# One gate of the recurrence in seven-product form before the first branch projection, and two gates of the second branch at other places

## The chip, the cores and the metric

The kernel runs on one core of a Trainium2 chip. The metric is device time in microseconds; the median of three runs of the kernel before is 935.56 us (934.21 to 936.03). The profile shows one more execution, which took 935.83 us; its span, from the first to the last instruction that the trace shows, is 933.7 us, so 2.1 us lie around it. Engines are named as in the profile: PE (matmuls), DVE (VectorE), ACT (ScalarE), POOL (GpSimd) and SP (which issues the weight loads).

## The reference

A decoder block over 512 tokens and 16 meta tokens in front of them, width 1024, all in float32. Cut to what matters here:

```python
u = rmsnorm(h, mix_norm_w)
q, k, v, g_ret, lru_in, lru_gate, gate_a, gate_b = split(u @ w_in)
o = chunk_retention(rotary(q), rotary(k), v)
y_ret = (silu(g_ret) * o) @ w_branch_ret
r = rg_lru(causal_depthwise_conv(lru_in), ...)
y_lru = (gelu(lru_gate) * r) @ w_branch_lru
mixed = sigmoid(gate_a) * y_ret + sigmoid(gate_b) * y_lru
h = h + mixed @ w_out
h = h + swiglu(rmsnorm(h, ffn_norm_w))
out = rmsnorm(h, final_norm_w)[:, 16:]
```

## The kernel before

Every float32 operand of a product is split in two halves: `hi`, the value cast to PE's fast 32-bit form (ACT, line 290 for weights, line 421 for activations), and `lo`, what the cast lost (DVE, line 294 or 422; a few on POOL). Each product is then three matmuls, hi by hi, hi by the other's lo, and lo by hi.

A weight slab of 1024 by 256 comes in four quarters of 128 partitions by 512 columns (a11, a12, a21, a22). There are two ways to multiply by it. `plain` uses the four quarters as they are: with 256 tokens per matmul that is 4 quarters x 2 token halves x 4 blocks x 3 matmuls = 96 matmuls. `fast` is a seven-product (Strassen-Winograd) form: POOL makes four sums of quarters, s1 to s4 (`combine`, line 260); seven operands (s1, s3, a12, a11, s4, a22, s2) are split by ACT and DVE; PE does 7 x 4 x 3 = 84 matmuls against the activations' quarters and their own sums t1 to t4, in four PSUM regions z, w, y, x; in the middle ACT copies w and x out and DVE adds z and w (`pz`, line 393), and at the end ACT copies x again (`u2`, line 398) and DVE makes the four output quarters by two additions (lines 407 and 408). `plain_slab` says which slabs take which way.

`PLAN` gives the order of the stages: R0 to R3 (the retention's projections), A0 to A3 (the gates of the first branch), I0 to I3 (the recurrence's inputs, followed by the convolution), L0 to L3 (the recurrence's output gates: a projection and a Gelu), T0 to T3 (the recurrence's inner gates and the recurrence itself), B0 to B3 (the gates of the second branch), BR and BL (the two branch projections). In the trace, a slab of `w_in` has a number: I0 and I1 are 16 and 17, L0 to L3 are 20 to 23, A0 to A3 are 24 to 27, B0 to B3 are 28 to 31. I0, I1 and the A gates are `fast`; I2, I3, all L and all B are `plain`.

A convolution (`conv`, line 978 and three lines 980 for each of two halves, on DVE) reads the padded input `xp` and writes `c`, which ACT and DVE then split (lines 421 and 422, 128x528); the work is issued bit by bit between the matmuls (`tick`). `branch` multiplies four activations R0 to R3 (or Z0 to Z3), each of 128x1024 and each split before use, by four slabs; BR is 192 matmuls of 512 columns in two groups of four PSUM banks (`w_br0_*`, `w_br1_*`). BR also gives back the activations' sums t1 to t4, so that nothing `fast` can follow it.

Three things set the order. Each engine runs its own queue strictly in the order of the built program; a scheduler has made that order at build time from the order of the code. Buffers are rings: 8 raw quarters, 9 pairs of hi and lo, 4 sums, 8 PSUM banks; a cast to `hi` waits until PE has read the pair nine places earlier. All larger tiles (named b with a number) live in 32 slots of SBUF that are handed out first freed, first used; a tile waits for the last reader of the tile that had its slot.

Of the kernel before, what the change touches and what calls it, by code (L numbers as in the profile page):

```python
# [13 lines left out]
AF = mybir.ActivationFunctionType  # L14
# [6 lines left out]
SEQ = 512  # L21
# [41 lines left out]
FIRST_LOADS = "w0 x1 w1 m w2 w3 x2 x3"  # L63


PLAN = "R0 R1 R2 R3 A0 A1 A2 A3 I0 I1 BR T0 L0 I2 T1 L1 I3 L2 T2 B0 L3 T3 B1 B2 B3 BL"

PLAIN_R = "K0 G0 K1 K2 K3".split()
NORM = 2.0
# [41 lines left out]
class Slots:  # L111
# [12 lines left out]
    def get(self, n=SEQ, dt=F32):  # L124
        if n <= T and dt == F32:
            if self.halves:
                slot, i = self.halves.pop(0)
            else:
                slot, i = [*self.open(dt), 0], 0
                self.halves.append((slot, 1))  # L130
            slot[2] += 1
            t = slot[1][:, i * T:i * T + n]
            self.held[id(t)] = (t, slot, i)
        else:
            tag, mem = self.open(dt)
            t = mem[:, :n]
            self.held[id(t)] = (t, tag, None)
        return t
# [15 lines left out]
def hybrid_block(ctx: ExitStack, tc: tile.TileContext, a: dict):  # L154
# [10 lines left out]
    def bank(name):  # L165
        return ps.tile([P, 512], F32, tag="ps", name=name)
# [24 lines left out]
    Q, K, V, G, LI, LG, GA, GB = (4 * i for i in range(8))  # L191
# [4 lines left out]
    SLAB_OF = {"I": ("w_in", LI), "L": ("w_in", LG), "A": ("w_in", GA), "B": ("w_in", GB), "T": ("gates", 0)}  # L196
    for step in PLAN.split():
        if step in ("BR", "BL"):
            order += [(f"w_{step.lower()}", hf) for hf in range(2)]
        elif step[0] == "R":  # L200
            s = int(step[1])
# [12 lines left out]

    def plain_slab(key, i):
        if key == "w_in":
            return i in [{"Q": Q, "K": K, "G": G}[r[0]] + int(r[1]) for r in PLAIN_R] or LI + 2 <= i < GA or i >= GB
        return key == "w_fi" and i <= FIRST

    pieces = []  # L220
    for n, (key, i) in enumerate(order):
        if n == 0:
            pieces += PLAIN_V
        if key in ("w_br", "w_bl"):

            pieces += [(key, k // 2, k % 2 + 2 * (1 - i)) for k in range(KT)]
        elif plain_slab(key, i):
            pieces += [(key, i, c) for c in PLAIN]
        elif key == "w_v":
            pieces += [(key, j, c) for c in FAST for j in (i, i + 1)] if i else []  # L230
        elif key in ("w_in", "w_fi"):
            pieces += [(key, i, c) for c in FAST]
        elif key == "w_fo":
            pieces += [(key, i, c) for c in (2, 0, 3, 1)]
        else:
            pieces += [(key, i, c) for c in range(2 if key == "gates" else 4)]
    state = {"n": 0, "look": 0}

    def behind(ins, other):

        if other is not None:
            tc.add_manual_dep(ins.ins, other.ins.name, mybir.DependencyInfo(
                mybir.DependencyClass.NoSync, mybir.DependencyReason.DATA), reason="issue order")
        return ins
# [74 lines left out]
    def lookup(*args, **kw):  # L319
        state["table"] = behind(nc.scalar.activation(*args, **kw), state.get("table"))  # L320
# [56 lines left out]
    def fast(key, s, X, n, banks, name):  # L377

        z, w_, y, x = banks
        own = n == TH
        ws = small.tile([P, TH], F32, tag="ws", name=f"ws{name}{s}")
        pz = small.tile([P, 2, TH], F32, tag="pz", name=f"pz{name}{s}")
        u2 = small.tile([P, TH], F32, tag="u2", name=f"u2{name}{s}")
        part = lambda name: weights((key, s, name))[0]
        block(z, part("s1"), X["t1"], n, True)
        block(w_, part("s3"), X["t3"], n, own)
        block(y, part("a12"), X["b21"], n, True)  # L390
        block(x, part("a11"), X["b11"], n, own)
        nc.scalar.copy(ws[:, :n], w_)
        nc.vector.tensor_tensor(pz[:, 1, :n], z, ws[:, :n], op=ALU.add)  # L393
        nc.scalar.copy(pz[:, 0, :n], x)  # L394
        block(z, part("s4"), X["b22"], n, False)
        block(w_, part("a22"), X["t4"], n, False)
        block(x, part("s2"), X["t2"], n, False)
        nc.scalar.copy(u2[:, :n], x)
        return pz, u2

    def fast512(key, s, X, out, name):

        zw, yx = bank(f"zw{name}{s}"), bank(f"yx{name}{s}")
        pz, u2 = fast(key, s, X, 256, (zw[:, :256], zw[:, 256:], yx[:, :256], yx[:, 256:]), name)
        out = out.rearrange("p (q n) -> p q n", n=256)
        halves = lambda t: t.rearrange("p (q n) -> p q n", n=256)
        nc.vector.tensor_tensor(out[:, 0::3], halves(yx), pz[:, :, :256], op=ALU.add)
        nc.vector.tensor_tensor(out[:, 1:3], halves(zw), u2[:, :256].unsqueeze(1).broadcast_to([P, 2, 256]), op=ALU.add)
# [25 lines left out]
    def plain(key, s, n, outs, X):  # L434


        shared = n == 256
        for j in range(2):
            for i, part in enumerate(PLAIN[2 * j:2 * j + 2]):
                w = weights((key, s, part))[0]  # L440
                for h in range(2):
                    block(outs[j][h], w, X[("b11", "b12", "b21", "b22")[2 * i + h]], n, i == 0 and (h == 0 or not shared))

    def plain512(s, name):

        pbs = [bank(f"{name}{s}_{j}") for j in range(2)]
        plain("w_in", s, 256, [(pb[:, :256], pb[:, 256:]) for pb in pbs], UV)
        return pbs
# [47 lines left out]
    def blocks_of(n):  # L496

        F = {b: get(4 * TH) for b in BLOCKS.values()}
        X = {b: (get(4 * TH, F32R), get(4 * TH, F32R)) for b in BLOCKS.values()}
        v4 = lambda t: t[:, :4 * n].rearrange("p (k t) -> p k t", k=4)  # L500
        return F, X, {b: v4(t) for b, t in F.items()}, {b: tuple(v4(t) for t in x) for b, x in X.items()}
# [40 lines left out]
    UF, U, UFV, UV = blocks_of(TH)  # L542
    for load in FIRST_LOADS.split():
        if load[0] == "w":
            key, i, c = pieces[int(load[1:])]
# [238 lines left out]
    def ret_project(s):  # L784
# [15 lines left out]
        if plain_slab("w_in", Q + s):  # L800
            rotate(q4, 256, [(j, slice(0, 2), pb) for j, pb in enumerate(plain512(Q + s, "q"))])
        else:
            fast512("w_in", Q + s, UV, q, "q")
            rotate(q4, 256)
        kk = get(2 * T)
        k4 = kk.rearrange("p (j n t) -> p j n t", j=2, n=2)
        if plain_slab("w_in", K + s):
            outs = [[bank(f"k{s}_{j}{n}")[:, :TH] for n in range(2)] for j in range(2)]
            plain("w_in", K + s, TH, outs, UV)
            rotate(k4, TH, [(j, slice(n, n + 1), outs[j][n]) for j in range(2) for n in range(2)])  # L810
        else:
            for j, n, pb, add in fast528("w_in", K + s, UV, "k"):
                nc.vector.tensor_tensor(k4[:, j, n], pb, add, op=ALU.add)
            rotate(k4, TH)
# [240 lines left out]

    def lru_gate(s):
        x = get(D)
        for j, pb in enumerate(plain512(LG + s, "lg")):
            lookup(x[:, j * SEQ:(j + 1) * SEQ], pb, AF.Gelu_apprx_tanh)
        Z[s] = x  # L1060


# [20 lines left out]

    plan = PLAN.split()
    for step in plan:
        s = int(step[1]) if step[1:2].isdigit() else None
# [251 lines left out]
```

## Time and profile before

| | |
|---|---|
| median of three runs | 935.56 us |
| the profiled execution | 935.83 us |
| its span | 933.7 us |
| DVE busy | 666.5 us, 71% of the span |
| ACT busy | 461.6 us, 49% |
| POOL busy | 333.2 us, 36% |
| BR's matmuls (`w_br`) start | 298.2 to 346.8 us |
| L0's matmuls (`lg`, first) start | 352.8 us |
| transfer of a quarter of `w_in`, issue to landing | 3.1 us (median of 112) |

The page divides the span by engine; a busy share over the whole span is a mean of stages with other limits, so the stage of the change, 280 to 350 us, is to be read by itself: in windows of 20 us and in the timeline of each engine, where the number in square brackets at a row's end is the idle time ahead of it and what ended it. A row of the timeline can stand for several like instructions (x2, x3); its second column is then their whole time. From the start of one to the start of the next is less than the duration shown, because instructions of one engine overlap a little.

### The profile page before, as it was taken

What the parts mean: (1) busy time and instruction counts of PE and PEld (TensorE: products, weight loads), DVE (VectorE), ACT (ScalarE), POOL (GpSimd) and SP (SyncE); (2) the same over time, 40 slices, a digit from 0 to 9 for tenths busy, and PEclk for the clock granted to TensorE, in tenths of its full rate; (3) what the DMA queues carried; (4) which work ended last, traced back from release to release, by engine and by line L of the source; (5) the groups of instructions that cost most, each with busy time, mean ns of one, the idle gap of its engine ahead of it and who ended that gap; (6) DMA issues with size and microseconds to landing.
All of it is one profiled execution on the core that took longest, in us unless ns stands there. A gap on an engine that the chain in (4) does not pass through costs nothing.

```text
span 933.7 us, 16985 instructions
## 1 busy us (share of the span) xinstructions
PE 918.5 (98%) x6610; PEld 864.0 (93%) x6610; DVE 666.5 (71%) x906; ACT 461.6 (49%) x817; POOL 333.2 (36%) x243
## 2 busy tenths in 40 slices
PE   8999999999999999999999999999999999999996
PEld 8999999998999889999998888999999999888885
DVE  5877977888788836777744527958999999842223
ACT  6653454554555337747933324545555556632213
POOL 5134634445351002102100214458787786000003
PEclk9999999999999999999999999999999999999999
DMA  7142123131124332233442222223223323433202
GB/s 279 49 136 84 52 94 110 36 113 46 62 82 139 108 104 75 90 112 90 147 128 91 91 90 91 71 84 116 93 92 120 107 91 116 145 115 100 79 1 91
DMA packets 48497, 91.50 MB, mean 98 GB/s; under 512 B 5520, under 2 KB 5648, under 8 KB 48416
## 3 DMA queue, kind: packets, MB, share of 16 engines
q1 hardware_dynamic: 46976, 86.70, 29.0%
q10 hardware_dynamic: 1440, 3.71, 1.3%
q8 instruction: 52, 0.85, 0.4%
q14 instruction: 29, 0.24, 0.1%
HBM read 88.29 MB, written 2.10 MB: 97 GB/s over the span
## 4 chain that ended last, share of the span: by engine, by line
PE 95%; DVE 3%; DMA 1%; issue 1%; POOL 0%; ACT 0%; POOLq 0%; DVEq 0%; SPq 0%
PE fo L364 4%; PE fo L362 4%; PE fo L363 4%; PE zwf L372 4%; PE zwf L373 4%; PE zwf L374 4%; PE yxf L374 3%; PE yxf L373 3%; PE yxf L372 3%; PE k L372 2%; PE k L374 2%; PE k L373 2%; PE lg L374 2%; PE gate L374 2%; PE gate L372 2%; PE lg L372 2%
## 5 line engine op out<-in xcount | busy, mean ns | idle before, releaser
L294 DVE TENSOR_TENSOR lo<-raw_w_in,hi 128x512 fp32r<-128x512 f32 x99 | 85.5, 869 | 37.0 <-ACT hi L290 34.9
L290 ACT CAST hi<-raw_w_in 128x512 fp32r<-128x512 f32 x99 | 60.8, 620 | 63.4 <-PE w_br L363 13.8
L372 PE MATMUL zwf<-b,hi 128*128 128x256 f32 x304 | 85.7, 283 | 0.6 <-DVE pzf L393 0.6
L294 DVE TENSOR_TENSOR lo<-s_w_fi,hi 128x512 fp32r<-128x512 f32 x76 | 76.0, 1027 | 13.1 <-ACT hi L290 9.3
L373 PE MATMUL zwf<-b,hi 128*128 128x256 f32 x304 | 85.0, 280 | 0.0
L374 PE MATMUL zwf<-b,lo 128*128 128x256 f32 x304 | 85.0, 280 | 0.0
L294 DVE TENSOR_TENSOR lo<-raw_w_fo,hi 128x512 fp32r<-128x512 f32 x44 | 30.2, 690 | 61.9 <-ACT hi L290 61.9
L364 PE MATMUL fo<-hi,b 128*128 128x512 f32 x176 | 69.5, 395 | 0.0
L362 PE MATMUL fo<-hi,b 128*128 128x512 f32 x176 | 69.1, 394 | 0.0
L363 PE MATMUL fo<-lo,b 128*128 128x512 f32 x176 | 69.1, 392 | 0.0
L260 POOL TENSOR_TENSOR s_w_fi<-raw_w_fi,raw_w_fi 128x512 f32<-128x512 f32 x38 | 64.1, 1704 | 6.2 <-DVE lo L294 4.7
L294 DVE TENSOR_TENSOR lo<-raw_w_fi,hi 128x512 fp32r<-128x512 f32 x47 | 64.4, 1397 | 1.0 <-ACT hi L290 0.8
L374 PE MATMUL yxf<-b,lo 128*128 128x256 f32 x228 | 63.3, 281 | 0.0
L373 PE MATMUL yxf<-b,hi 128*128 128x256 f32 x228 | 63.3, 280 | 0.0
L372 PE MATMUL yxf<-b,hi 128*128 128x256 f32 x228 | 62.1, 280 | 0.2 <-ACT pzf L394 0.2
L290 ACT CAST hi<-raw_w_fo 128x512 fp32r<-128x512 f32 x44 | 27.3, 620 | 68.7 <-PE fo L364 63.7
L294 DVE TENSOR_TENSOR lo<-s_w_in,hi 128x512 fp32r<-128x512 f32 x52 | 49.8, 962 | 14.0 <-ACT hi L290 11.8
L372 PEld LDWEIGHTS zwf<-b,hi 128*128 128x128 f32 x304 | 57.0, 188 | 2.4 <-DVE pzf L393 2.4
L290 ACT CAST hi<-s_w_fi 128x512 fp32r<-128x512 f32 x76 | 45.8, 618 | 26.0 <-PE zwf L373 15.0
L290 ACT CAST hi<-raw_w_fi 128x512 fp32r<-128x512 f32 x69 | 42.0, 619 | 32.5 <-PE yxf L373 16.5
L374 PEld LDWEIGHTS zwf<-b,lo 128*128 128x128 f32 x304 | 57.4, 189 | 0.0
L373 PEld LDWEIGHTS zwf<-b,hi 128*128 128x128 f32 x304 | 57.3, 188 | 0.0
(380 smaller groups left out, 3305.8 us busy)
## 6 DMA issues: line engine op xcount, KB each, us to landing
raw_w_in<-in_w_in SPq DMA_DIRECT2D x112, 256.0 KB, 3.1
raw_w_fi<-in_w_fi SPq DMA_DIRECT2D x88, 256.0 KB, 3.4
raw_w_fo<-in_w_fo SPq DMA_DIRECT2D x44, 256.0 KB, 3.0
raw_w_v<-in_w_v SPq DMA_DIRECT2D x16, 256.0 KB, 4.6
raw_w_br<-in_w_br SPq DMA_DIRECT2D x16, 256.0 KB, 3.2
raw_w_bl<-in_w_bl SPq DMA_DIRECT2D x16, 256.0 KB, 3.2
raw_w_out<-in_w_out SPq DMA_DIRECT2D x16, 256.0 KB, 2.9
b<-in_x SPq DMA_DIRECT2D x4, 512.0 KB, 6.5
```

What stands on the lines that cost most here:

```text
L260: behind(nc.gpsimd.tensor_tensor(sums[key, i, name], x, y, op=op), state.get("diag"))
L290: nc.scalar.copy(hi, src)
L294: engine.tensor_tensor(lo, src, hi.bitcast(F32), op=ALU.subtract)
L362: nc.tensor.matmul(out, wh, xh, start=start, stop=False, skip_group_check=True)
L363: nc.tensor.matmul(out, wh, xl, start=False, stop=False, skip_group_check=True)
L364: nc.tensor.matmul(out, wl, xh, start=False, stop=stop, skip_group_check=True)
L372: nc.tensor.matmul(out, wh, xh, start=start and i == 0, stop=False, skip_group_check=True)
L373: nc.tensor.matmul(out, wh, xl, start=False, stop=False, skip_group_check=True)
L374: nc.tensor.matmul(out, wl, xh, start=False, stop=i == 3, skip_group_check=True)
```

## The change

L0 moves ahead of BR and takes the seven-product form; its Gelu then runs once over 128x1024 in SBUF instead of twice over 128x512 in PSUM. B0 takes L0's old place behind T0, and B1 goes ahead of T3, so that two gates instead of three stand between T3 and BL. Nothing else is edited.

```diff
-PLAN = "R0 R1 R2 R3 A0 A1 A2 A3 I0 I1 BR T0 L0 I2 T1 L1 I3 L2 T2 B0 L3 T3 B1 B2 B3 BL"
+PLAN = "R0 R1 R2 R3 A0 A1 A2 A3 I0 I1 L0 BR T0 B0 I2 T1 L1 I3 L2 T2 L3 B1 T3 B2 B3 BL"
...
-            return i in [{"Q": Q, "K": K, "G": G}[r[0]] + int(r[1]) for r in PLAIN_R] or LI + 2 <= i < GA or i >= GB
+            return i in [{"Q": Q, "K": K, "G": G}[r[0]] + int(r[1]) for r in PLAIN_R] or (LI + 2 <= i < GA and i != LG) or i >= GB
...
     def lru_gate(s):
         x = get(D)
-        for j, pb in enumerate(plain512(LG + s, "lg")):
-            lookup(x[:, j * SEQ:(j + 1) * SEQ], pb, AF.Gelu_apprx_tanh)
+        if plain_slab("w_in", LG + s):
+            for j, pb in enumerate(plain512(LG + s, "lg")):
+                lookup(x[:, j * SEQ:(j + 1) * SEQ], pb, AF.Gelu_apprx_tanh)
+        else:
+            fast512("w_in", LG + s, UV, x, "lg")
+            lookup(x, x, AF.Gelu_apprx_tanh)
         Z[s] = x
```

What it moves in the queues shows at three places. On PE, before, BR's first matmuls follow I1's (`xli17`); their activation R0 is split in b86 (hi) and b87 (lo):

```order
L374 MATMUL xli17_3797<-b10_114,lo129_3700 128x264
L362 MATMUL w_br0_0_3954<-b86_3958,hi133_3768 128x512
L363 MATMUL w_br0_0_3954<-b87_3959,hi133_3768 128x512
L364 MATMUL w_br0_0_3954<-b86_3958,lo133_3769 128x512
L362 MATMUL w_br0_1_3955<-b86_3958,hi133_3768 128x512
```

On PE, after the change, BR begins behind all of I1 and all 84 matmuls of L0 (`zwlg20`, `yxlg20`); R0 is split in b90 (hi) and b91 (lo):

```order
L374 MATMUL yxlg20_3958<-b30_562,lo139_3914 128x256
L362 MATMUL w_br0_0_4110<-b90_4114,hi140_3931 128x512
L362 MATMUL w_br0_1_4111<-b90_4114,hi140_3931 128x512
L362 MATMUL w_br0_2_4112<-b90_4114,hi140_3931 128x512
L362 MATMUL w_br0_3_4113<-b90_4114,hi140_3931 128x512
L362 MATMUL w_br1_0_4280<-b90_4114,hi148_4120 128x512
L362 MATMUL w_br1_1_4281<-b90_4114,hi148_4120 128x512
L362 MATMUL w_br1_2_4282<-b90_4114,hi148_4120 128x512
L362 MATMUL w_br1_3_4283<-b90_4114,hi148_4120 128x512
L363 MATMUL w_br0_0_4110<-b91_4115,hi140_3931 128x512
```

So eight hi-by-hi matmuls on R0 now stand ahead of the first that reads R0's lo, and each of them reads b90. On ACT, before, R0's cast to b86 stands among the casts for A2 (slab 26):

```order
L320 ACTIVATE b74_2967<-b74_2967 128x1024
L421 CAST b86_3958<-b40_922 128x1024
L898 ACTIVATE b75_3017<-o7_3214 128x512
L290 CAST hi107_3240<-raw_w_in26_3_3160 128x512
```

On ACT, after the change, R0's cast to b90 is the last of L0's tail, behind L0's copy `u2lg`, its Gelu (b86 is now L0's output) and the casts of I1's convolution (b87 to b88):

```order
L398 COPY u2lg20_3961<-yxlg20_3958 128x256
L320 ACT_TABLE_LOAD
L320 ACTIVATE b86_3956<-b86_3956 128x1024
L421 CAST b88_3972<-b87_3971 128x528 x2
L421 CAST b90_4114<-b40_922 128x1024
L290 CAST hi149_4138<-raw_w_br0_1_4136 128x512
```

The split moved because of its slot: in the built program b90 lies at the address of b82, the padded input of I1's convolution, and so cannot be written before that convolution's last line 980 has read b82. On DVE, before, R0's lo stands at A3's casts (slab 27), 28 rows ahead of I0's additions of `xli16`:

```order
L843 TENSOR_TENSOR b72_2800<-oT6_3445,b72_2800 128x512
L422 TENSOR_TENSOR b87_3959<-b40_922,b86_3958 128x1024
L294 TENSOR_TENSOR lo117_3439<-raw_w_in27_1_3331,hi117_3438 128x512
```

On DVE, after the change, this is the end of the queue that leads to BR (b82 to b87 is I1's convolution, b93 and b95 are the lo halves of R1 and R2):

```order
L422 TENSOR_TENSOR b93_4155<-b50_1442,b92_4154 128x1024
L980 SCALAR_TENSOR_TENSOR b87_3971<-b82_3807,vec_70,b87_3971 128x526
L294 TENSOR_TENSOR lo148_4121<-raw_w_br0_0_4118,hi148_4120 128x512
L422 TENSOR_TENSOR b95_4195<-b64_2319,b94_4194 128x1024
L407 TENSOR_TENSOR b86_3956<-yxlg20_3958,pzlg20_3960 128x2x256
L408 TENSOR_TENSOR b86_3956<-zwlg20_3957,u2lg20_3961 128x512
L980 SCALAR_TENSOR_TENSOR b87_3971<-b82_3807,vec_70,b87_3971 128x525 x2
L422 TENSOR_TENSOR b89_3973<-b87_3971,b88_3972 128x528 x2
L422 TENSOR_TENSOR b91_4115<-b40_922,b90_4114 128x1024
```

The last two lines 980 of I1's convolution, the last that read b82, stand behind L0's two output additions, and R0's lo behind them. Between I0's additions (`xli16`, `zli16`, `wli16`) and that second line 980 stand, after the change: 14 lines 294 (`lo135` to `lo148`), 4 lines 978, 12 lines 980, 2 lines 393, 4 pairs of lines 959 and 960, 2 lines 422 of 128x528 and 3 of 128x1024, and lines 407 and 408 once each.

On POOL the four sums of slab 20 come right behind those of slab 17, where the queue was empty before until T0. On SP the four loads of slab 20 come behind those of slab 17 and ahead of BR's sixteen; those of slab 28 take slab 20's old place.

## The prediction

> **What bounds the kernel now.** First the page's span and busy times, then the list of who waited for whom for PE alone, then windows of 20 and 40 us.
>
> ```profile
> span 933.7 us, 16985 instructions
> PE 918.5 (98%) x6610; PEld 864.0 (93%) x6610; DVE 666.5 (71%) x906; ACT 461.6 (49%) x817; POOL 333.2 (36%) x243
> ...
> PE zwg L372 <- DVE pzg L393: 2.3, 1, 2.3
> ...
> 280.00:300.00 20.00, 20.00 (x160) 19.70 (x159) 15.56 (x30) 12.24 (x23) 3.16 (x2) 1.00 0.43 135
> 300.00:320.00 20.00, 20.00 (x106) 17.05 (x105) 19.00 (x34) 7.30 (x13) 0.00 (x0) 1.00 0.39 124
> ...
> 400.00:420.00 20.00, 20.00 (x168) 20.00 (x168) 15.10 (x25) 8.63 (x17) 1.65 (x1) 1.00 0.37 117
> ...
> 520.00:560.00 40.00, 40.00 (x174) 32.49 (x174) 15.76 (x20) 10.70 (x16) 8.96 (x8) 1.00 0.27 87
> ```
>
> PE is the bound: 918.5 of 933.7 us, and in the stage of the change it never stands still. So a matmul that goes is a gain of its pitch: 20/168 = 0.119 us with 256 columns, 40/174 = 0.230 with 512. But the same windows show the second thing to see: from 300 to 320 us DVE is busy 19.00 of 20. PE is not held there, because BR's matmuls need little of what DVE is late with. Whatever makes PE wait for the end of DVE's queue at that place costs PE time in full.
>
> **What PE saves.** L0 takes 84 matmuls instead of 96: 12 x 0.119 = 1.43 us. B0's move and B1's leave PE's work as it is.
>
> **What PE then waits for.** Before, R0 was split long before BR: its hi on ACT at 252.06, its lo on DVE at 269.25, and BR's first matmul came at 298.25 without a wait.
>
> ```profile
> 252.06 1.03 ACT L421 CAST b<-b 128x1024 fp32r<-128x1024 f32 x1
> 269.25 2.00 DVE L422 TENSOR_TENSOR b<-b,b 128x1024 fp32r<-128x1024 f32 x1
> 298.25 0.40 PE L362 MATMUL w_br<-b,hi 128*128 128x512 f32 x1
> ```
>
> After the change, BR's first eight matmuls read b90. Its cast stands on ACT behind two casts of I1's convolution, and these need the convolution's last two lines 980, which stand on DVE behind L0's output additions. So PE must wait for DVE's whole queue down to the second of them. I price that queue from the rows of the same operations before, start to next start:
>
> ```profile
> 285.40 0.68 DVE L407 TENSOR_TENSOR b<-yxgate,pzgate 128x512 f32<-128x512 f32 x1
> 286.01 0.68 DVE L408 TENSOR_TENSOR b<-zwgate,u2gate 128x512 f32<-128x512 f32 x1
> ...
> 294.01 0.69 DVE L294 TENSOR_TENSOR lo<-raw_w_br,hi 128x512 fp32r<-128x512 f32 x1 [0.82 <-PE zli L374]
> 294.62 0.42 DVE L959 TENSOR_TENSOR b<-xli,pzli 128x256 f32<-128x256 f32 x1
> 294.95 0.16 DVE L960 TENSOR_TENSOR b<-xli,pzli 128x8 f32<-128x8 f32 x1
> 295.02 0.42 DVE L959 TENSOR_TENSOR b<-zli,u2li 128x256 f32<-128x256 f32 x1
> ...
> 295.83 0.68 DVE L294 TENSOR_TENSOR lo<-raw_w_br,hi 128x512 fp32r<-128x512 f32 x1
> 296.43 1.01 DVE L978 TENSOR_SCALAR b<-b,vec 128x528 f32<-128x528 f32 x2
> 297.36 0.68 DVE L294 TENSOR_TENSOR lo<-raw_w_br,hi 128x512 fp32r<-128x512 f32 x1
> 297.96 0.76 DVE L980 SCALAR_TENSOR_TENSOR b<-b,vec,b 128x527 f32<-128x527 f32 x1
> 298.64 0.42 DVE L393 TENSOR_TENSOR pzli<-zli,wsli 128x264 f32<-128x264 f32 x1
> 298.99 0.75 DVE L980 SCALAR_TENSOR_TENSOR b<-b,vec,b 128x527 f32<-128x527 f32 x1
> ...
> 304.83 1.23 DVE L422 TENSOR_TENSOR b<-b,b 128x1024 fp32r<-128x1024 f32 x1 [0.17 <-PE wli L374]
> 305.97 1.29 DVE L294 TENSOR_TENSOR lo<-raw_w_br,hi 128x512 fp32r<-128x512 f32 x2
> 307.18 2.46 DVE L422 TENSOR_TENSOR b<-b,b 128x528 fp32r<-128x528 f32 x3
> 309.55 0.68 DVE L294 TENSOR_TENSOR lo<-raw_w_br,hi 128x512 fp32r<-128x512 f32 x1
> ```
>
> A line 294 takes 0.605 (285.40 to 286.01 shows the same pitch for lines 407 and 408); 978 takes 0.465; 980 takes 0.67; 393 takes 0.35; a pair 959 and 960 takes 0.40; 422 takes 1.14 for 128x1024 and 0.615 for 128x528 (307.18 to 309.55 is one of the first and two of the second). With the counts of the section on the change, from the first line 294 after I0's additions (295.83 before) to the convolution's last line 980:
>
> 14 x 0.605 + 4 x 0.465 + 12 x 0.67 + 2 x 0.35 + 4 x 0.40 + 2 x 0.615 + 3 x 1.14 + 2 x 0.605 = 8.47 + 1.86 + 8.04 + 0.70 + 1.60 + 1.23 + 3.42 + 1.21 = 26.5 us.
>
> Its start cannot be earlier, since the line 294 at 294.01 waits for PE by way of a cast. It can be later: POOL now makes L0's sums between 284 and 295, and a line 294 beside POOL's sums is slow (the pair at 218.58, quoted below, took 1.77 each). I take 0.4 us, between nothing (the 0.82 of waiting swallows it) and 1.2 (one such line). So DVE is done at 295.83 + 0.4 + 26.5 = 322.7. Then, on ACT:
>
> ```profile
> 305.38 1.17 ACT L421 CAST b<-b 128x528 fp32r<-128x528 f32 x2
> 306.45 0.61 ACT L290 CAST hi<-raw_w_br 128x512 fp32r<-128x512 f32 x1
> 306.97 1.05 ACT L421 CAST b<-b 128x1024 fp32r<-128x1024 f32 x1
> ...
> 347.59 1.28 ACT L320 ACT_TABLE_LOAD   x1
> ```
>
> one cast of 128x528 (1.07/2 = 0.54) and the cast to b90 (1.05); the hand-overs between engines are left out. PE may start BR at 324.3. The Gelu and its table load (1.28) fit ahead: the load comes while DVE is still at its queue, and the Gelu (bounded by the 1.05 of a 128x1024 cast) beside the last lines 980, 1.34 us.
>
> Without waits, PE would come to BR at 298.25 + 84 x 0.119 + the 36 matmuls of I1 that BR's used to surround, 36 x 0.123 (264 columns, 0.119 x 264/256) = 298.25 + 10.0 + 4.4 = 312.6. **So PE waits 324.3 - 312.6 = 11.7 us.** About 1 us of it comes earlier, inside L0, where its second half needs the line 393 `pzlg`, 18 rows into that queue; since DVE runs without a stop, the sum is the same wherever PE waits. DVE itself waits for nobody here: the last cast it needs from L0's end, `u2lg`, is possible at about 314, when DVE still has 6 us of older work. R0's lo comes 1.2 us behind the cast, beside the eight hi-by-hi matmuls (1.84 us), and costs nothing. Bounds of the wait: 10.9 (the start 0.4 earlier, DVE's pitches 1.5% shorter, about what my reading of them can be off) to 12.5 (the start at its later bound).
>
> **What the wait does to PE's clock.** The same kind of wait, in G3's slab:
>
> ```profile
> 218.58 3.53 DVE L294 TENSOR_TENSOR lo<-raw_w_in,hi 128x512 fp32r<-128x512 f32 x2
> ...
> 222.50 0.39 PE L372 MATMUL zwg<-b,hi 128*128 128x256 f32 x1 [2.27 <-DVE pzg L393]
> ...
> 224.00 0.41 PE L374 MATMUL zwg<-b,lo 128*128 128x256 f32 x1
> 224.22 0.41 PE L372 MATMUL zwg<-b,hi 128*128 128x256 f32 x1
> ...
> 222.50:223.00 0.50, 0.50 (x4) 0.50 (x5) 0.50 (x2) 0.00 (x0) 0.00 (x0) 0.98 0.00 0
> 223.00:223.50 0.50, 0.50 (x5) 0.50 (x4) 0.50 (x4) 0.00 (x0) 0.31 (x1) 0.50 0.52 160
> ...
> 226.00:226.50 0.50, 0.50 (x5) 0.50 (x5) 0.28 (x1) 0.00 (x0) 0.09 (x1) 0.60 0.52 156
> ```
>
> After 2.27 us without work the granted clock was 0.50 from 223.0 to 226.4, and the pitch 0.21 instead of 0.119: 16 matmuls lost 0.093 each, 1.5 us. A wait of over 10 us will do the same to BR: 3.4 us at half pace lose about 1.6 us (bounds 0.8, if the clock returns within half that time, and 3.1, if it needs twice as long). The 1 us inside L0 may do it too, and then at no cost: PE is ahead of DVE until BR begins.
>
> [...]
>
> **What costs nothing.** POOL's four sums lie where its queue was empty. The loads on SP come in another order, with the same bytes, in a stage where DMA is busy 0.35 to 0.43. Three more casts, the copies of L0's middle and three DVE additions are in the queues already counted, or on ACT, which is busy 7.30 of 20 there. B0 in L0's old place is the same `plain` slab with one table load. The gain of DVE's emptier queue behind BR is worth nothing, since PE waited nowhere between 280 and 560.
>
> **The sum:** 11.7 + 1.6 - 1.43 = +11.9 us. The profiled execution goes from 935.83 to 947.7; its own time is 0.27 us above the median of the runs, 935.56, and on that median it is **947.5 us, 1.3% slower**.
>
> **The rivals.**
>
> *The change does what it says, and is not slower.* If R0's cast stood on ACT before PE gets to 312.6, only the 1.43 us would be left: 934.1 us, within 0.2% of before (about what a measurement of this kernel can tell from no change). It decides at a DVE queue of 312.6 - 296.2 - 1.6 = 14.8 us instead of 26.5. For it: PE had no wait with DVE at 19.00 of 20. Against it: that was with R0 split 50 us earlier. Chance 4%, a quarter of it or less beyond 0.2%.
>
> *Part of the queue.* PE waits for L0's own line 393, but the slot binds less than the order says; with half the wait, 5.9 + 1.5 - 1.43, it is 941.5 us. Against it: the queue is strictly in order. Chance 4%.
>
> *More than this wait.* [...]
>
> ```profile
> 452.96 0.53 ACT L320 ACTIVATE b<-gt,vec 128x264 f32<-128x264 f32 x1
> 473.23 1.22 DVE L422 TENSOR_TENSOR b<-b,b 128x1024 fp32r<-128x1024 f32 x1 [1.11 <-ACT b L421]
> ```
>
> From T3's last sigmoid to Z3's lo it took 474.45 - 452.96 = 21.5 us. The two gates give 192 x 0.119 = 22.8, and BL comes to Z3 only 72 matmuls of 512 later, 16.6 us. That covers it unless BL's own weight splits, now among the recurrence on DVE, come late; 3 us of that with a half clock once more would give 935.56 + 11.9 + 3 + 1.6 = 952.1. Chance of the two together 10%.
>
> **How the numbers follow.** The forecast has 82%: 945.8 to 949.7 by its bounds (10.9 + 0.8 - 1.43 and 12.5 + 3.1 - 1.43). To hold 8 in 10 with a part of the dearer case and some room below, the range is 944.5 to 951.0. Slower by over 0.2%: 82 + 4 + 10 = 96%, of which I give 1 back for what I have not seen: 95%. Within 0.2%: 4%. Faster: 1%.
>
> **What would show it.** In the profile after: a row of PE on `w_br` at about 313 to 325 us with some 10 us of idle time ahead of it, released by ACT's line 421; about 1 us on `zwlg`, released by line 393; DVE without a gap between 296 and 322; a granted clock of 0.50 for some 3.4 us behind it; 84 matmuls on L0; no wait on `w_bl`. Wrong would be: BR's first matmul at 313 without idle time, DVE idle in that stretch, or a whole clock behind a 10 us wait.

## The result and the profile after

The changed kernel takes 948.76 us (median of 4 runs, 947.17 to 949.45) where the kernel before took 935.79 beside it (934.21 to 936.07): the ratio is 1.0137, with a 95% interval from 1.0125 to 1.0149, so 13.0 us and 1.4% slower. The forecast was 947.5.

The page of the profiled execution (947.17 us), span and busy time by engine:

```profile
span 944.9 us, 16985 instructions
PE 919.3 (97%) x6598; PEld 863.5 (91%) x6598; DVE 668.0 (71%) x912; ACT 464.3 (49%) x822; POOL 337.7 (36%) x247
```

PE has 12 matmuls fewer than before and is busy 0.8 us longer, and the span is 11.2 us longer. So the loss is idle time, and a little pace. The list of what PE waited for, in total, times and longest, has two entries above 0.2 us that the kernel before does not have:

```profile
PE w_br L362 <- ACT b L421: 10.6, 1, 10.6
...
PE zwlg L372 <- DVE pzlg L393: 0.9, 1, 0.9
```

The timelines of DVE, ACT and PE in that stage (start, duration, in brackets the idle time ahead and what ended it):

```profile
294.47 0.69 DVE L294 TENSOR_TENSOR lo<-raw_w_in,hi 128x512 fp32r<-128x512 f32 x1
...
318.44 0.72 DVE L407 TENSOR_TENSOR b<-yxlg,pzlg 128x512 f32<-128x512 f32 x1
319.04 0.72 DVE L408 TENSOR_TENSOR b<-zwlg,u2lg 128x512 f32<-128x512 f32 x1
319.64 1.47 DVE L980 SCALAR_TENSOR_TENSOR b<-b,vec,b 128x525 f32<-128x525 f32 x2
...
319.79 1.06 ACT L320 ACTIVATE b<-b 128x1024 f32<-128x1024 f32 x1 [4.37 <-DVE b L408]
320.75 2.09 ACT L421 CAST b<-b 128x528 fp32r<-128x528 f32 x3
...
322.90 3.78 PE L362 MATMUL w_br<-b,hi 128*128 128x512 f32 x8 [10.57 <-ACT b L421]
```

This is read from the bottom up. BR's first eight matmuls start at 322.90, after 10.57 us of idle time. They were released by a line 421 on ACT: the last of the three casts that begin at 320.75, which is R0's. The two ahead of it are the convolution's; they follow DVE's last two lines 980, which end at 321.1. And DVE ran from 294.47 to there without a gap, 26.6 us.

Windows of 20 us, then three of half a us, show the pace (length, then busy time of PE, PEld, DVE, ACT and POOL with their counts, the granted clock, DMA share, GB/s):

```profile
300.00:320.00 20.00, 11.44 (x94) 11.03 (x92) 20.00 (x35) 11.68 (x20) 0.00 (x0) 0.92 0.41 131
320.00:340.00 20.00, 17.10 (x66) 13.85 (x67) 6.43 (x9) 5.68 (x9) 0.00 (x0) 0.82 0.16 49
...
323.00:323.50 0.50, 0.50 (x2) 0.40 (x3) 0.50 (x1) 0.00 (x0) 0.00 (x0) 0.50 0.00 0
326.50:327.00 0.50, 0.50 (x3) 0.40 (x2) 0.00 (x0) 0.00 (x0) 0.00 (x0) 0.50 0.00 0
327.00:327.50 0.50, 0.50 (x4) 0.42 (x3) 0.00 (x0) 0.00 (x0) 0.00 (x0) 0.99 0.00 0
```

The granted clock is 0.50 until 327.0. PE works from 322.9, so 4.1 us of BR's work ran at half pace and lost 2.05 us. The sum of the stage is 0.88 + 10.57 + 2.05 - 1.43 = 12.1 us. The spans differ by 11.2, and in this execution G3's wait did not cost the half clock that it cost before (the last section). From I0's first matmul to BL's first, a stretch that lies behind G3, PE took 219.9 us (276.2 to 496.1) instead of 207.5 (277.8 to 485.4): 12.4 us more, so all but 0.3 us of the stage is accounted for.

In experiments 5, 8 and 10 one execution took far longer than the others (1291.89, 1024.69 and 5130.07 us), and the ratios leave these out.

### The profile page after: what moved, and what is told of

It reads as the page before. It is cut to its first block, busy times and chain, and to the rows that moved or that the text cites. A ratio compares the mean times of both kernels' runs of the same rounds, so it can differ in the third digit from the quotient of the medians.

```text
span 944.9 us, 16985 instructions
## 1 busy us (share of the span) xinstructions
PE 919.3 (97%) x6598; PEld 863.5 (91%) x6598; DVE 668.0 (71%) x912; ACT 464.3 (49%) x822; POOL 337.7 (36%) x247
## 4 chain that ended last, share of the span: by engine, by line
PE 90%; DVE 5%; DMA 1%; issue 1%; POOL 1%; ACT 1%; POOLq 0%; SPq 0%; DVEq 0%; ACTq 0%
PE fo L364 4%; PE fo L362 4%; PE fo L363 4%; PE zwf L372 4%; PE zwf L374 4%; PE zwf L373 4%; PE yxf L374 3%; PE yxf L373 3%; PE yxf L372 3%; DVE lo L294 2%; PE w_br L362 2%; PE gate L374 2%; PE gate L372 2%; PE gate L373 2%; PE wo L364 2%; PE w_br L363 2%
## 5 line engine op out<-in xcount | busy, mean ns | idle before, releaser
L294 DVE TENSOR_TENSOR lo<-raw_w_in,hi 128x512 fp32r<-128x512 f32 x98 | 81.7, 840 | 35.5 <-ACT hi L290 33.2
L294 DVE TENSOR_TENSOR lo<-s_w_fi,hi 128x512 fp32r<-128x512 f32 x76 | 74.3, 1005 | 13.7 <-ACT hi L290 9.6
L294 DVE TENSOR_TENSOR lo<-s_w_in,hi 128x512 fp32r<-128x512 f32 x56 | 55.4, 989 | 16.1 <-ACT hi L290 15.9
L290 ACT CAST hi<-s_w_in 128x512 fp32r<-128x512 f32 x56 | 34.7, 620 | 52.7 <-PE zwgate L373 11.6
L260 POOL TENSOR_TENSOR s_w_in<-raw_w_in,raw_w_in 128x512 f32<-128x512 f32 x28 | 39.3, 1406 | 58.2 <-DVE lo L294 38.9
L372 PEld LDWEIGHTS zwf<-b,hi 128*128 128x128 f32 x304 | 56.9, 188 | 2.2 <-DVE pzf L393 1.3
```

What stands on the lines that cost most here:

```text
L260: behind(nc.gpsimd.tensor_tensor(sums[key, i, name], x, y, op=op), state.get("diag"))
L290: nc.scalar.copy(hi, src)
L294: engine.tensor_tensor(lo, src, hi.bitcast(F32), op=ALU.subtract)
L372: nc.tensor.matmul(out, wh, xh, start=start and i == 0, stop=False, skip_group_check=True)
```

## The experiments

All ratios are to the kernel before, run on the same chip beside each, with the 95% interval.

**1. R0's parts in another slot.** The slot that I1's padded input gave back stands first in the list when BR takes its tiles. One line puts it last.

```diff
+            slots.free.append(slots.free.pop(0))
             branch("w_br", lambda i: R[i], gated(macc, GA))
```

> The changed kernel with one line more: just ahead of BR the free slot that I1's padded input left is put at the end of the list, so that R0's two parts take another address. In its program R0's cast now stands on ACT ahead of the last two u2lg copies, the table load and the Gelu, and PE issues 24 of BR's matmuls ahead of L0's last 36. Theory (the slot ties R0's cast behind the last two L980 of I1's conv, which stand at the end of DVE's queue): the 10.6-us wait at w_br goes; what may be left is up to 3 us later in BR, where R1's remainder still stands behind L407, L408 and the last L980 on DVE. Time 934 to 940 us, 936.5 the likeliest, the granted clock whole through the stage. Rival (the slot is beside the point: DVE has 26 us of work ahead of BR, and BR can't be fed before it is done, whichever R is first): the wait comes back inside BR, 8 to 11 us in all, 945 to 949 us.

Measured: 934.73 us beside 934.99, ratio 0.9998 (0.9988 to 1.0007). The loss of 13 us is gone with this line. PE's one new wait, the last row of L980 on DVE's timeline, and the windows:

```profile
PE w_br L362 <- DVE b L407: 0.3, 1, 0.3
...
322.23 0.75 DVE L980 SCALAR_TENSOR_TENSOR b<-b,vec,b 128x525 f32<-128x525 f32 x1
...
300.00:320.00 20.00, 20.00 (x136) 18.44 (x135) 20.00 (x37) 12.86 (x22) 0.00 (x0) 1.00 0.43 136
320.00:340.00 20.00, 19.70 (x86) 15.77 (x85) 10.64 (x17) 7.25 (x11) 0.00 (x0) 1.00 0.33 104
```

The telling row is the one of DVE: its last line 980 starts at 322.23, later than the 321.1 at which it was finished in the changed kernel, and DVE is busy 20.00 of 20 us. DVE is as late as ever, and PE no longer depends on it. The rival (DVE's work must be done in any slot) falls. The line does more than move an address: the program's order follows the tie, and here BR's first matmuls start at 307.42, while L0's last end at 317.4. So the run weighs the tie together with the order that it forces; the same holds of experiments 7, 11 and 12, and experiment 8 tells the two apart.

**2. Less on DVE, with the slot as it was.** The remainders of BR's weights are computed on POOL.

```diff
-ON_POOL = {"w_fi": ("a22",), "w_out": (1, 3)}
+ON_POOL = {"w_fi": ("a22",), "w_out": (1, 3), "w_br": (0, 1, 2, 3)}
```

> The changed kernel with the 16 remainders of BR's weights (lo, L294) computed on POOL instead of DVE; the slots are as in the changed kernel. Theory (what PE waits for is the end of DVE's queue ahead of R0's cast): nine L294 of 0.605 us leave the stretch ahead of the last L980, 5.4 us, and in this program L407, L408 and three L422 stand behind it instead of ahead, another 4.8 us, so the cast can start about 10 us earlier and the wait ahead of BR falls from 10.6 to under 1 us; R0's remainder, fifth of the L422 that follow, and the lo on POOL (1.5 us each there) may hold BR for 2 to 5 us more. Time 936 to 942 us. Rival 1 (the wait belongs to the slot and not to how much DVE has to do): as the changed kernel, 948 to 949 us. Rival 2 (POOL becomes the bound: 9 lo of 1.5 us behind the sums of L0's weights): PE waits at w_br on POOL instead of ACT, 945 us or more.

Measured: 948.21 us beside 934.99, ratio 1.0139 (1.0125 to 1.0153). The expectation of 936 to 942 failed, and by the time alone the first rival would have won. The waits and the timelines of POOL and DVE say something else:

```profile
PE zwlg L372 <- DVE pzlg L393: 5.3, 1, 5.3
PE w_br L363 <- DVE b L422: 2.7, 1, 2.7
PE w_br L362 <- ACT b L421: 1.2, 1, 1.2
...
303.32 6.36 POOL L294 TENSOR_TENSOR lo<-raw_w_br,hi 128x512 fp32r<-128x512 f32 x4 [10.26 <-ACT hi L290]
309.90 3.22 POOL L294 TENSOR_TENSOR lo<-raw_w_br,hi 128x512 fp32r<-128x512 f32 x2 [0.23 <-ACT hi L290]
...
301.82 0.75 DVE L980 SCALAR_TENSOR_TENSOR b<-b,vec,b 128x526 f32<-128x526 f32 x1
303.09 4.19 DVE L980 SCALAR_TENSOR_TENSOR b<-b,vec,b 128x526 f32<-128x526 f32 x3
307.20 0.41 DVE L959 TENSOR_TENSOR b<-xli,pzli 128x256 f32<-128x256 f32 x1
308.42 1.55 DVE L978 TENSOR_SCALAR b<-b,vec 128x528 f32<-128x528 f32 x1
311.92 1.76 DVE L980 SCALAR_TENSOR_TENSOR b<-b,vec,b 128x527 f32<-128x527 f32 x1
313.61 0.41 DVE L393 TENSOR_TENSOR pzlg<-zwlg,wslg 128x256 f32<-128x256 f32 x1
```

The wait for R0's cast fell from 10.6 to 1.2 us, but mostly because PE came to it 8 us later: L0's last matmul ends at 320.4 instead of 312.3, and BR begins at 321.60 instead of 322.90. While POOL works, from 303.3 to 313.1, DVE's lines 980 and 978 take 1.5 to 1.8 us instead of 0.75 and 0.55 (of the three in the row at 303.09, the first took 0.76 and the others 1.8). That delays `pzlg` to 313.61, and PE waits 5.3 us for it inside L0. DVE's last line 980 ended at 318.0, 3.1 us earlier than in the changed kernel, but R0's cast on ACT stood behind a weight's cast that waited for L0's matmuls until 318.9. What DVE gained was taken back by other waits; this run does not decide between the theories, and experiments 9 and 10 were made for that.

**3. The place without the form.** L0 stays plain (96 matmuls) at its new place.

```diff
-(LI + 2 <= i < GA and i != LG)
+LI + 2 <= i < GA
```

> The changed kernel with L0 left in the plain form (96 matmuls and no sums, pzlg, L407 and L408), in the new place ahead of BR; B0 and B1 as in the changed kernel. It tells the place from the form. Theory (place, slot and queue): R0's cast is still behind the last two L980; DVE has about 3.4 us less ahead of them, PE arrives 1.4 us later, so PE waits about 6 us ahead of BR, with up to 2 us of half clock behind it: 941 to 946 us, 943.5 the likeliest. Rival (the seven-product form is the cost: the form alone takes the DVE and ACT time that PE waits for): within 1 us of the kernel before, 935 to 937 us.

Measured: 946.07 us beside 934.99, ratio 1.0119 (1.0105 to 1.0132). The place alone costs 11.1 us; the form is not the cause. The wait and what stands ahead of it:

```profile
PE w_br L362 <- ACT b L421: 7.0, 1, 7.0
...
315.85 4.14 DVE L980 SCALAR_TENSOR_TENSOR b<-b,vec,b 128x527 f32<-128x527 f32 x6
319.35 2.25 ACT L421 CAST b<-b 128x528 fp32r<-128x528 f32 x3 [3.65 <-DVE b L980]
...
320.00:340.00 20.00, 18.34 (x70) 14.78 (x71) 5.91 (x8) 4.68 (x7) 0.00 (x0) 0.83 0.17 53
```

It is the same pattern, the last line 980 and then three casts, with a wait of 7.0 us, a us more than expected. PE is idle only 1.66 us of the last window and yet does 70 matmuls where a full one has 88: 18 x 20/88 = 4.1 us, of which 2.4 are the half clock. In the trace 9.5 us of the loss lie between I0's first matmul and BL's first (217.0 us instead of 207.5), near 7.0 + 2.4; the rest lies outside the stage, as in experiment 8.

**4. The gate alone.** B0 and B1 at their old places.

```diff
-... I0 I1 L0 BR T0 B0 I2 T1 L1 I3 L2 T2 L3 B1 T3 B2 B3 BL
+... I0 I1 L0 BR T0 I2 T1 L1 I3 L2 T2 B0 L3 T3 B1 B2 B3 BL
```

> The changed kernel with B0 and B1 at their old places: L0's new place and form alone. Theory: the two B gates cost nothing and bring nothing, their neighbours on PE being as long as before; so the time of the changed kernel, 947.5 to 949.5 us, with the same wait of 10 to 11 us at w_br. Rival (the moved B gates have a part in the loss, by what they shift on DVE and in the loads behind): 2 us or more under the changed kernel, below 947 us.

Measured: 948.25 us, ratio 1.0143 (1.0129 to 1.0157), with the same waits of 10.6 and 0.9 us. L0 carries the whole loss.

**5. The clock held through the wait.** In the form's function, behind its last product, for L0 alone:

```diff
+        if name == "lg":
+            idle = bank("idle")[:, :n]
+            for i in range(7):
+                block(idle, last, X["t2"], n, True)
```

> The changed kernel with 84 more matmuls of 256 columns, whose sums nothing reads, behind L0's own: 39 ahead of its last 36 and 45 ahead of BR (0.119 us each, 4.6 and 5.4 us). They fill the two waits of 0.9 and 10.6 us and leave everything else in its place. Theory (after the wait PE works at half pace from 322.9 to 327.0, which costs 2.05 us): the granted clock stays whole from 300 to 340, BR starts when it did, and the time falls by about 2 us, to 946 to 947.5 us. Rival (the half clock behind the wait costs nothing, since BR then waits for something else, or PE has no half clock to lose): 948 to 949.5 us, as the changed kernel; above that if the matmuls themselves are in the way.

Measured: 945.13 to 946.38 us beside 934.94, ratio 1.0112 (1.0096 to 1.0127). That is 10.5 us above the kernel before, where the changed kernel's 1.0137 is 12.8: about 2.3 us less, give or take 1.8 by the two intervals. Rows of DVE and PE (in this kernel the convolution's line 980 is line 985), and the windows:

```profile
319.64 0.76 DVE L985 SCALAR_TENSOR_TENSOR b<-b,vec,b 128x525 f32<-128x525 f32 x1
...
323.42 1.08 PE L362 MATMUL w_br<-b,hi 128*128 128x512 f32 x4
...
300.00:320.00 20.00, 20.00 (x170) 20.00 (x169) 19.13 (x37) 10.01 (x19) 0.00 (x0) 1.00 0.39 121
320.00:340.00 20.00, 19.55 (x100) 16.28 (x99) 10.13 (x14) 8.49 (x11) 0.00 (x0) 1.00 0.26 80
```

The clock stayed whole, as the theory says. But the edit did not leave the rest in its place, so the size of the gain can't be put down to the clock alone. In this program one line 294, two lines 422 and lines 407 and 408 fall behind the convolution's last line, which ends 23.5 us behind the queue's first line 294 (296.88 to 320.40) instead of 26.6. BR then began 26.5 us behind that line (at 323.42, when the added matmuls were through) where the changed kernel has 28.4 (294.47 to 322.90), 1.9 us sooner, and waited 0.45 us later on. What the half clock costs rests on the trace of the changed kernel, 2.05 us.

**6. The two B gates alone**, in the kernel before.

```diff
-... I0 I1 BR T0 L0 I2 T1 L1 I3 L2 T2 B0 L3 T3 B1 B2 B3 BL
+... I0 I1 BR T0 L0 B0 I2 T1 L1 I3 L2 T2 L3 B1 T3 B2 B3 BL
```

> The kernel before with B0 and B1 alone in the changed kernel's places; L0 plain and behind T0. Theory (the two gates move without cost): the time of the kernel before within 0.2%, 933 to 937 us. Rival (they cost or bring something that the loss ahead of BR hides): 1% away on either side.

Measured: 935.49 us beside 934.94, ratio 1.0001 (0.9992 to 1.0010). They cost nothing that can be measured, and BL never waits for T3.

**7. The same slot, given to R3.**

```diff
+            slots.free.insert(6, slots.free.pop(0))
             branch("w_br", lambda i: R[i], gated(macc, GA))
```

> The changed kernel with the slot of I1's padded input given to R3's hi, which BR needs last, instead of R0's, which it needs first; everything else as in the first experiment. Theory (a cast in that slot can't start before the last L980, at 321 to 323 us; what that costs is PE's need of it): R3 is wanted only behind some 90 of BR's and L0's matmuls, at about 324 us, so the wait is at most 1.5 us: 934 to 938 us. Rival (whichever input of BR has the slot, its cast holds the casts behind it on ACT, those of BR's weights among them, and PE with them): 3 us or more of waits, over 939 us.

Measured: 934.82 us beside 934.94, ratio 0.9992 (0.9983 to 1.0001), without a wait on `w_br`. The slot's former reader is as late as before, on DVE and ACT:

```profile
322.51 0.75 DVE L980 SCALAR_TENSOR_TENSOR b<-b,vec,b 128x525 f32<-128x525 f32 x1
...
323.74 1.57 ACT L421 CAST b<-b 128x528 fp32r<-128x528 f32 x2
```

The pair of casts at 323.74 is the convolution's second and, behind it, R3's. One input of BR is ready only at 325.3, and that costs nothing, because PE does not want it sooner. What was paid for in the changed kernel is not the slot as such, but its going to the tile that is read first.

**8. The place without the form, with the slot out of the way**: experiment 3 with the line of experiment 1.

> The third experiment (L0 plain, ahead of BR) with the slot moved as in the first. It tells whether the place alone costs anything once the slot is out of the way. Theory: no; 96 matmuls as before and no wait over 1 us, so the kernel before's time, 934 to 938 us, the third experiment's 7.0-us wait at w_br gone. Rival (with I1's conv on DVE ahead of BR, its inputs come late in any slot): a wait of 3 us or more at w_br, 939 us or more.

Measured: 936.23 to 938.53 us beside 934.94, ratio 1.0023 (1.0013 to 1.0033), and no wait on `w_br`. Of the 11.1 us of experiment 3 all but about 2 are gone. BR stands behind all of L0 here, as in experiment 3: L0's last matmul starts at 314.62, there at 314.35. DVE's last line 980 ends at 323.0, 3 us later than there (320.0), and still the wait of 7.0 us is gone. So it was the slot, and not BR's place among L0's matmuls. The rest is more than the theory's nothing. The trace has PE busy without a gap from 280 to 360 us, and from I0's first matmul to BL's first it takes 207.4 us, as before (207.5), so the rest does not lie in the stage. The profiled span is 2.4 us longer than before's: 0.7 us ahead of I0's first matmul, 0.9 from BL's first to PE's last and 0.9 behind that. What it is stays open.

**9 and 10. A longer and a shorter queue behind the same slot.** In I1's convolution the last tap is added three times (first line), or only one tap is added (second line):

```diff
-            for i in range(1, 4):
+            for i in (1, 2, 3, 3, 3) if b == 1 else (1, 2, 3):
+            for i in range(1, 2 if b == 1 else 4):
```

> The changed kernel with the last tap of I1's convolution added three times instead of once, so with four more L980 (0.67 us each) on DVE ahead of R0's cast and nothing else moved. Theory (the wait at w_br is set by the end of DVE's queue): the last L980 ends 2.7 us later, the wait grows from 10.6 to 13.3 us, and the time by 2.7 us against the changed kernel's 948.8 (1.4% above the kernel before), give or take the 1 us that the half clock behind the wait can shift: 950.5 to 952.5 us. Rival (something other than DVE's queue, such as the loads of BR's weights, releases PE about then): under 950 us, the wait at 10.6.

Measured: 951.41 us beside 934.57, ratio 1.0171 (1.0157 to 1.0185). Four lines 980 of 0.67 us make 2.7 us, and the wait grew from 10.6 to 13.2:

```profile
PE w_br L362 <- ACT b L421: 13.2, 1, 13.2
...
321.98 4.17 DVE L980 SCALAR_TENSOR_TENSOR b<-b,vec,b 128x525 f32<-128x525 f32 x6
327.81 2.50 PE L362 MATMUL w_br<-b,hi 128*128 128x512 f32 x5 [13.15 <-ACT b L421]
```

DVE's queue has the changed kernel's order here, with the four added lines at its end. This shows the second half of the theory with nothing else moved: the end of DVE's queue sets the wait, us for us.

> The changed kernel with only the last tap but two of I1's convolution left (two taps of four are out), so with four L980 less on DVE; in this program three L294, three L422, L407 and L408 also fall behind R0's cast. R0's parts keep the slot of I1's padded input. Theory: DVE's work from the first L294 behind I0's additions to the last L980 is 17.5 us instead of 26.6, so R0's cast can start at 312 and BR at 313.6, one to two us after PE comes to it; up to 3 us more may be waited for R0's remainder. Time 935 to 940 us with the slot tie in place. Rival (the tie itself or the seven-product form costs, and not the length of the queue): 945 us or more.

Measured: 945.65 us beside 934.57, ratio 1.0107 (1.0092 to 1.0123), where 935 to 940 was expected. By the time, the rival would stand; the trace shows two steps that the expectation missed. The largest wait, then rows of DVE's, ACT's and PE's timelines and the windows:

```profile
PE w_br L362 <- ACT b L421: 3.3, 1, 3.3
...
312.89 0.79 DVE L980 SCALAR_TENSOR_TENSOR b<-b,vec,b 128x527 f32<-128x527 f32 x1
314.50 1.04 ACT L421 CAST b<-b 128x1024 fp32r<-128x1024 f32 x1
315.45 0.36 ACT L398 COPY u2lg<-yxlg 128x256 f32<-128x256 f32 x1
315.71 1.57 ACT L421 CAST b<-b 128x528 fp32r<-128x528 f32 x2
317.34 2.43 PE L362 MATMUL w_br<-b,hi 128*128 128x512 f32 x6 [3.33 <-ACT b L421]
320.26 1.36 PE L362 MATMUL w_br<-b,hi 128*128 128x512 f32 x2 [0.49 <-DVE b L407]
322.52 0.80 PE L363 MATMUL w_br<-b,hi 128*128 128x512 f32 x1 [0.90 <-DVE b L422]
...
300.00:320.00 20.00, 15.56 (x114) 14.14 (x112) 20.00 (x37) 14.10 (x23) 0.00 (x0) 0.95 0.41 131
320.00:340.00 20.00, 18.84 (x66) 14.67 (x67) 5.92 (x9) 4.16 (x6) 0.00 (x0) 0.79 0.19 60
```

First, DVE's work took the 17.5 us that were expected (296.16 to 313.68; the stage began 1.7 us later than in the changed kernel's profile, and PE came to BR as much later). But R0's cast, the second of the pair at 315.71, stood behind a weight's cast, another input's cast and a copy of L0's end on ACT, so BR began at 317.34 and not at 315.3, where the two casts alone would have put it. The wait for the slot fell from 10.6 to 3.3 us all the same. Second, from 320 to 340 PE is idle 1.16 us and does 66 matmuls instead of 88: 5.0 us are missing, 3.8 of them by the half clock. Short waits in a row, 3.3 and then 0.5 and 0.9, cost more in clock here than the one long wait: PE worked 8.8 us at half pace (4.4 us lost) where the changed kernel has 4.1. With the 0.9 us inside L0 the waits make 5.6 us, and 5.6 + 4.4 - 1.43 = 8.6; the trace has 9.2 from I0's first matmul to BL's first (216.7 instead of 207.5). So the rival is not needed: the loss is what is left of the wait for the slot, two shorter waits behind it and the half clock.

**11 and 12. What is left of the saving.** The eleventh is the fourth with the slot given to R3, the twelfth the seventh once more.

> The fourth experiment (L0's new place and form alone, B0 and B1 at their old places) with the slot given to R3 as in the seventh. It asks whether anything of the 12 matmuls (1.43 us) that L0 saves is left once the slot is out of the way. Theory (all of it, as no wait takes its place): 1.4 us under the kernel before, 0.15%, so 0.998 to 0.999. Rival (it is given back in smaller pieces, as the first and the seventh experiment suggest, 0.1 to 0.3 us under the kernel before): 0.999 to 1.000.

> The seventh experiment's kernel once more, beside the eleventh on one chip, for the same question: the seventh's ratio was 0.9992, from 0.9983 to 1.0001. Theory: 0.998 to 0.999. Rival: 0.999 to 1.000.

Measured, beside 936.02 us: 934.17, ratio 0.9987 (0.9978 to 0.9996), and 934.14, ratio 0.9983 (0.9974 to 0.9991). Both intervals lie below 1: with the slot moved, the change makes the kernel faster than before, by 1.2 and 1.6 us in 936. The 12 matmuls are worth 1.43. The traces say the same: from I0's first matmul to BL's first PE takes 206.2 and 205.9 us where the kernel before takes 207.5. The gain is small beside the scatter: the twelfth's kernel, measured as the seventh, has 0.9992 with an interval that just reaches 1, and the first experiment's has 0.9998.

## Why the prediction was right, point by point

- **PE's saving, 1.43 us.** PE's count fell from 6610 to 6598. What the saving is worth was seen only once the slot was moved: 1.3 and 1.6 us in the traces of experiments 11 and 12.
- **The cause: the slot ties R0's cast to the end of DVE's queue.** Shown from four sides: another slot takes the loss away (1), the same slot costs nothing for a tile that is wanted later (7), the loss is there without the form (3), and the wait follows the queue's length upward (9: 2.7 us of work, 2.6 of wait). Downward it fell too, from 10.6 to 3.3 us, by less than DVE's work, since ACT then held the cast (10). In 1 and 7 BR also begins ahead of L0's end on PE; 8 takes the wait away without that, and 9 lengthens the queue with every engine's order as it was.
- **The queue, 26.5 us.** It ran 26.6 us without a gap.
- **Its start.** I had added 0.4 us for POOL's sums. POOL's sums lay ahead of the queue's lines 294 (the last began at 289.86) and slowed none of them (0.69 to 0.72 us each), so the reason was wrong. The slow pair that I quoted, 1.77 us each from 218.58, stood beside POOL's line 648 (218.83 to 221.56) and not beside its sums; beside a sum (223.19 to 224.47) one took 1.22. Still the queue's first line 294 came 18.3 us behind I0's first matmul, where before it came 18.0 behind it; why is open. That the allowance fits is luck. In absolute times everything lay earlier than forecast, since I0's first matmul came at 276.2 instead of 277.8 in this execution.
- **The wait, 11.7 us, about 1 us of it inside L0.** 10.57 + 0.88 = 11.45. Against I0's first matmul DVE's queue ended as forecast, the hand-overs that I had left out took 0.2 us, and PE without waits would have come to BR 0.5 us later than I thought. In the trace `pzlg` is the 28th instruction of the queue and not 18 rows into it, as I wrote; the wait for it was near the 1 us forecast.
- **The clock, 1.6 us.** The mechanism was right, the size too small: 2.05 by the trace. (Experiment 5 shows the clock held, but does not measure this term.) I had let the half clock last 3.4 us from PE's return, as behind G3's wait; it lasted 4.1. This is the term that was mis-sized, inside its bounds of 0.8 to 3.1. With it the sum is 11.45 + 2.05 - 1.43 = 12.1, where the trace has 12.4 from I0's first matmul to BL's first. The measured 13.0 is 0.9 more than the sum, within the scatter of the medians: 1.9 us lie between the fastest and the slowest run of the kernel before, 2.3 for the kernel after.
- **What was to cost nothing.** The B gates did (6, and 4 beside the changed kernel). No wait on `w_bl` appeared. DMA's share in the stage before was 0.26 to 0.43 and not 0.35 to 0.43; nothing hung on it.
- **The rivals.** "Does what it says" needed a cast ahead of 312.6, and experiments 1, 7 and 12 are that rival come true, by a line of code: the forecast for it was 934.1 us. "Part of the queue" fell. "More than this wait" did not come: no wait on `w_bl`, and though the half clock lasted longer than the 3.4 us taken, 10.2 us (316.8 to 327.0), PE was idle for 6.1 of them.

## What to carry to other kernels

When tiles come from a list of free slots, moving a stage also changes which tile inherits which slot, so look up whose last reader each tile of the critical engine now waits for. Here it paid to give a slot whose reader was still queued to the tile that is read last, or to a later tile, and not to the one that is read first. An engine can be full and harmless: what counts is whether the bound engine depends on the end of its queue or the middle.

## What the runs showed of the hardware

**In these runs the half clock came in pieces of near 3.4 us.** In half-us windows the granted clock is 1.00 or 0.50 but at the edges, so a window's time at half pace is (1 - clock)/0.5 of it. From the 20-us windows: the kernel after has 3.2 + 7.2 = 10.4 us, experiment 3 has 6.8, experiment 10 has 2.0 + 8.4 = 10.4, and here are the rows of experiment 9, and of the stretch of G3's wait in experiments 7 and 12:

```profile
320.00:340.00 20.00, 12.19 (x42) 9.76 (x43) 10.15 (x14) 4.77 (x7) 0.00 (x0) 0.66 0.12 36
...
220.00:240.00 20.00, 17.75 (x139) 17.26 (x138) 15.11 (x25) 8.30 (x16) 8.33 (x6) 0.91 0.22 71
...
220.00:240.00 20.00, 17.77 (x147) 17.03 (x147) 16.11 (x28) 9.44 (x18) 8.52 (x7) 1.00 0.25 80
```

The first row gives 13.6 us, the second 3.6. All are near 1, 2, 3 or 4 times 3.4 us. Added up over the half-us windows of each unbroken stretch at half pace it is 3.4 us (the kernel before), 6.8 (experiments 2 and 3), 10.2 (the kernel after, experiments 4 and 10) and 13.7 (experiment 9). In the kernel before, a wait of 2.27 us brought the half clock; in the kernel after, the wait of 0.88 us inside L0 did not (1.00 until 316.5). In experiment 10 PE was at work again from 317.34, with waits of 0.49 and 0.90 us, and was granted the half clock from 318.0 to 328.2, 10.2 us. So in these runs a wait's cost in clock did not follow from its length alone: 2.05 us lost behind the wait of 10.57 us, 4.4 behind those of 3.3, 0.5 and 0.9.

**The same wait cost clock in one execution and not in another.** The last two rows are one and the same kernel, run twice, with a wait of 2.2 us in that stretch both times. In the one execution PE was granted the half clock behind it and did 139 matmuls in the window, in the other the clock stayed whole and it did 147. The kernels before and after differ there in the same way, and the starts of the same matmuls give the price: from the first behind the wait to the first of `zwgate`, a stretch of equal work, it is 7.17 us in the kernel before (222.50 to 229.67, with the half clock) and 5.66 in the kernel after (222.35 to 228.01, without it), so 1.5 us. Of the 14 profiles of this study 8 have the half clock there and 6 do not, the kernel before among the 8 and the kernel after among the 6. That is as large as what the change saves. The runs of one kernel scatter with the granted clock as well: of the 23 of the kernel before beside experiment 11, the 7 with a mean clock of 0.998 took 933.97 to 934.66 us, the 6 with 0.994 935.94 to 936.86.

**POOL slowed some of DVE's operations and not others.** In experiment 2, lines 980 and 978, whose tile operands are all in SBUF, took 1.5 to 1.8 us beside POOL's line 294 (303.3 to 313.1) instead of 0.75 and 0.55; line 959, which reads PSUM, took 0.41 there (307.20), as at 301.41 with POOL idle. Why the one is slowed and the other not, no run shows.
